# A decoder block on one core: at the end of a plain weight group, the next operands' preparation is queued behind the operation that empties the group's first bank, and one operand fewer is loaded ahead there

## The chip, the cores and the metric

The kernel runs on one core of a Trainium2 chip. The metric is the device time of one execution in microseconds (us), the median of three runs. Engines are named as in the profile: PE is TensorE (matmuls), DVE is VectorE, ACT is ScalarE, POOL is GpSimd, SP is the engine that issues the weight transfers.

## The reference, cut to what matters

One decoder block over 256 tokens of width 2048, all in float32: a norm, one combined input projection, two mixers (gated linear attention in 4 heads, a gated short convolution) whose outputs are gated and merged, an output projection, and a gated feed-forward part of width 5632, both with a residual.

```python
h = rmsnorm(x, mix_norm_w)
q, k, v, g_out, gk_low, gate_b, gate_c, xc, merge_a, merge_b = split(h @ w_in)
y_a = rmsnorm(gla_chunked(q, k, v, log_g)) * silu(g_out)          # per head
y_b = gate_b * causal_depthwise_conv(gate_c * xc, conv_w)
x = x + (sigmoid(merge_a) * y_a + sigmoid(merge_b) * y_b) @ w_out
gate, up = split(rmsnorm(x, ffn_norm_w) @ w_gate_up)
x = x + (silu(gate) * up) @ w_down
out = rmsnorm(x, final_norm_w)
```

## The kernel before, in words

**Arithmetic.** Every float32 operand is split into a high part hi (rounded to the format fp32r) and a remainder lo, and each product of two operands is three matmuls: lo with hi, hi with lo, hi with hi (`mm3`, lines 366 to 370; the profile's rows at L368, L369 and L370). The 256 tokens are two tiles of 128, t = 0 and t = 1; a matmul has one token tile's activations as weights and 512 output columns of the weight matrix as the moving operand. One such 512-wide matmul starts 0.23 us after the one before.

**Pieces.** The weight matrices come in pieces of 512 KB (128 x 1024 numbers). `load_piece` traces for one piece its transfer on SP (L253 or L316), the cast to hi on ACT (`high`, L259) and, one piece later, the subtraction that gives lo on DVE (`low`, L264). PE needs both before it can start on the piece.

**Groups.** Weight blocks go in two kinds of groups. A plain group (`eights`; `down` for the down projection) takes the pieces as they are: each piece is multiplied first with token tile 0 (6 matmuls into one PSUM bank), then with token tile 1 (6 matmuls into another). A sevens group (`sevens`) takes two blocks together and gets along with 7 products in place of 8; for that DVE also adds blocks of weights (L280 raw<-y,x; L286 x<-x,...; a cast and a subtraction follow for such a sum as for any piece) and in the end combines five banks (v, u at L446 to L460). The pieces of a plain group and of a sevens group take turns in the stream.

**Names of groups.** In the mixer part: q, k, v; g, ma, gb, mb with a column block 0 to 3 for the gates (g_out, merge_a, gate_b, merge_b, all plain groups), gc for the sevens of gate_c with xc. Then wo0 to wo3 (output projection), fg and fu (gate and up, blocks 0 to 10; blocks 3 to 7, 9 and 10 in sevens, the others plain), dn0_0 to dn3_4 (down projection; the first number is the part of the hidden width, the second the column block).

**Banks.** Five of the eight PSUM banks belong to the sevens. The three others ("lent") go round among the plain groups: a group takes two and gives them back at its end. Its successor so gets the third bank for t = 0, and for t = 1 the bank that held the predecessor's t = 0. The successor's first matmul for t = 1, which comes 6 matmuls after its first for t = 0, has to wait until that bank has been emptied. What empties a bank is the group's `done`: a silu on ACT for g (L1024), a sigmoid on ACT and a multiplication on DVE for ma and mb (L1014, L1015), an addition to the residual on DVE for wo and, in `down`, for dn (L1199), a silu on ACT for fg (L1155), a multiplication on DVE for fu (L1158).

**Order.** Within an engine the scheduler sets the order by the place at which an operation is traced, by its own estimate of when operands are there, and by explicit constraints. `take` (line 356) is called for each piece in the order of the stream: it traces the loading of further pieces until LOOK = 5 beyond the piece that is used, then the piece's matmuls are traced. So the preparation of later pieces stands in the trace ahead of the `done` of the group whose last piece is being used. There are 5 buffers for raw, 6 for hi, 5 for lo, 2 for x and 1 for y.

Of the kernel before, what the change touches and what calls it, by code (L numbers as in the profile page):

```python
# [12 lines left out]
ALU = mybir.AluOpType  # L13
# [55 lines left out]
PARTS = ((0, 3), (3, 6), (6, 9), (9, 11))  # L69
# [122 lines left out]
def stream_list():  # L192

    pieces = [(p[0], p[3]) for p in piece_list()]
    out = [e for e in pieces if e[0] in ("k0", "q0", "v0")] + heads_list() + gates_list()
    out += [e for e in pieces if e[0] == "wo0"]
    return out + hidden_list() + down_list()
# [3 lines left out]
def block_kernel(ctx, tc, x, xt, cols_in, gkw_in, gku_in, gnw, conv_w, finw, w_in, w_out, w_gu, w_dn, out):  # L201
    nc = tc.nc
# [12 lines left out]
    def bank(shape, name, tag=None):  # L215

        if tag is None:
            tag = f"b{turn['b'] % turn['of']}"
            turn["b"] += 1
        return psum.tile(shape, F32, tag=tag, name=name)  # L220
# [16 lines left out]
    LOOK = 5  # L237
    stream = stream_list()
# [6 lines left out]
    count = {"loaded": 0, "used": 0, "tick": 0}  # L245
    pending = []
    held = {}
# [8 lines left out]
    def high(raw, piece, a=0, b=None):  # L256
        hi, n = piece[0], piece[2]
        ks = slice(a, b or n)
        nc.scalar.copy(hi[:, ks, :], raw[:, ks, :])  # L259

    def low(raw, piece, a=0, b=None):
        hi, lo, n = piece
        ks = slice(a, b or n)
        nc.vector.tensor_tensor(out=lo[:, ks, :], in0=raw[:, ks, :], in1=hi[:, ks, :].bitcast(F32), op=ALU.subtract)  # L264

    def sum_of(pair, what, q):

        one, two = pair
        if what == "21":
            return fetch(one, 4 * q + 2)  # L270
        if what == "22":
            return fetch(two, 4 * q + 2)
        if what == "11":
            held["y"] = fetch(one, 4 * q, held["pool"], "y")
            return held["y"]
        y = held["y"]
        if what == "t1":
            held["x"] = fetch(two, 4 * q, held["pool"], "x")
            raw = wraw.tile([P, 2, 512], F32, tag="raw", name="raw")
            nc.vector.tensor_tensor(out=raw, in0=y, in1=held["x"], op=ALU.add)  # L280
            return raw
        x = held["x"]
        if halfway and halfway[-1][0] is x:
            finish_low()
        other = y if what == "t2" else fetch(two if what == "t3" else one, 4 * q + 2)
        nc.vector.tensor_tensor(out=x, in0=x, in1=other, op=ALU.add)  # L286
        return x

    def load_piece():


        i = count["loaded"]
        count["loaded"] += 1
        if i < len(stream):
            key, k0 = stream[i]
            if isinstance(k0, tuple):
                n, w = 2, 512
                raw = sum_of(key, *k0)
                step = n
            else:  # L300
                mat, j, n, w = index[(key, k0)]
                raw = wraw.tile([P, n, w], F32, tag="raw", name="raw")

                step = n // 2 if i < 2 else n
            piece = [whi.tile([P, n, w], F32R, tag="hi", name="hi"), None, n]
            if isinstance(k0, tuple):
                high(raw, piece)
                halfway.append((raw, piece, key, k0))
            else:
                if i < 2:  # L310
                    piece[1] = wlo.tile([P, n, w], F32R, tag="lo", name="lo")
                for a in range(0, n, step):
                    b = a + step
                    if (i, a) in hooks:
                        hooks.pop((i, a))()
                    nc.sync.dma_start(  # L316
                        raw[:, a:b, :], mats[mat][j, :, a * w:b * w].rearrange("p (k c) -> p k c", c=w))
                    high(raw, piece, a, b)
                    if i < 2:
                        low(raw, piece, a, b)  # L320
                if i < 2:
                    ready[(key, k0)] = piece
                else:
                    halfway.append((raw, piece, key, k0))
        if len(halfway) > 1 or (halfway and i >= len(stream)):
            finish_low()

    def finish_low():
        raw, piece, key, k0 = halfway.pop(0)
        piece[1] = wlo.tile([P, piece[2], PIECE // piece[2]], F32R, tag="lo", name="lo")  # L330
        low(raw, piece)
        ready[(key, k0)] = piece
# [19 lines left out]
    def one_at_a_time(delay, fn):  # L352

        spaced.append((count["tick"] + delay, fn))

    def take(key, k0):
        while count["loaded"] <= len(stream) and count["loaded"] <= count["used"] + LOOK:
            load_piece()
        return ready.pop((key, k0))

    def used(n=1):
        count["used"] += n
        for _ in range(n):
            tick()
# [7 lines left out]
    def tok_piece(ps, t, piece, k0, first, last, a):  # L372
        hi, lo, n = piece
        for k in range(n):
            ah, al = a(t, k0 + k)
            mm3(ps, ah, al, hi[:, k, :], lo[:, k, :], first and k == 0, last and k == n - 1)
# [19 lines left out]
    def eights(key, a, done, tags=None):  # L396

        mine = tags or [lent.pop(0) for _ in range(NT)]
        ps = [bank([P, 512], f"{key}_{t}", tag) for t, tag in enumerate(mine)]
        for k0 in range(0, KC, 2):  # L400
            piece, _ = yield
            for t in range(NT):
                tok_piece(ps[t], t, piece, k0, k0 == 0, k0 == KC - 2, a)

                if k0 == KC - 2:
                    done(t, ps[t])
        if tags is None:
            lent.extend(mine)

# [664 lines left out]
    order = heads_list()  # L1074
# [86 lines left out]
    order = hidden_list()  # L1161
# [25 lines left out]
    def down(key):  # L1187

        part, n = (int(s) for s in key[2:].split("_"))
        cs = slice(DOWN[part][n][0], sum(DOWN[part][n]))  # L1190
        mine = [lent.pop(0) for _ in range(NT)]
        ps = [bank([P, cs.stop - cs.start], f"{key}_{t}", tag) for t, tag in enumerate(mine)]
        number = sum(e[0] == key for e in order)
        for i in range(number):
            piece, k0 = yield
            for t in range(NT):
                tok_piece(ps[t], t, piece, k0, i == 0, i == number - 1, hidden_act(part))
                if i == number - 1:
                    nc.vector.tensor_tensor(out=h[:, t, cs], in0=ps[t], in1=h[:, t, cs], op=ALU.add)  # L1199
        lent.extend(mine)  # L1200

    def hidden(key):
# [41 lines left out]
    order = down_list()  # L1244
# [15 lines left out]
    for e in order:  # L1260
        key, k0 = e
# [85 lines left out]
```

## Time and profile before

| | before |
|---|---|
| median of 3 runs | 1505.42 us (1503.13 to 1505.94) |
| the profiled execution | 1505.51 us, its span 1503.7 us |
| PE busy | 1485.7 us, 99% of the span |
| DVE busy | 1310.4 us, 87% |
| ACT busy | 873.3 us, 58% |
| DMA | 241 GB/s on average |
| TensorE clock granted | full in all 40 slices |

Lines of the profile give an operation's line in the kernel, its engine, its tile "out<-in" without buffer numbers, the shapes, how many there are and how long they took; "idle before <-X" says how long the engine stood before it and what ended that. A timeline row begins with the start and the length in us from the start of the span; rows of one kind that follow directly on each other are one row, with x2 and their common length. A matmul's length in the timeline (0.39 us) is longer than the distance to the next, since matmuls overlap. The span of 1503.7 us is the profiled part; 1.8 us of the execution's 1505.51 lie around it.

### The profile page before, as it was taken

What the parts mean: (1) busy time and instruction counts of PE and PEld (TensorE: products, weight loads), DVE (VectorE), ACT (ScalarE), POOL (GpSimd) and SP (SyncE); (2) the same over time, 40 slices, a digit from 0 to 9 for tenths busy, and PEclk for the clock granted to TensorE, in tenths of its full rate; (3) what the DMA queues carried; (4) which work ended last, traced back from release to release, by engine and by line L of the source; (5) the groups of instructions that cost most, each with busy time, mean ns of one, the idle gap of its engine ahead of it and who ended that gap; (6) DMA issues with size and microseconds to landing.
All of it is one profiled execution on the core that took longest, in us unless ns stands there. A gap on an engine that the chain in (4) does not pass through costs nothing.

```text
span 1503.7 us, 19400 instructions
## 1 busy us (share of the span) xinstructions
PE 1485.7 (99%) x7040; PEld 1239.4 (82%) x7040; DVE 1310.4 (87%) x1314; ACT 873.3 (58%) x993; POOL 33.0 (2%) x59
## 2 busy tenths in 40 slices
PE   9999999999999999999999999999999999999998
PEld 8989988888788788888888888888888788888887
DVE  7898878978988989966789999999998999999975
ACT  7755565654565565554556756655564556565553
POOL 0010000001001001000000000000000000000000
PEclk9999999999999999999999999999999999999999
DMA  9666677787786778787666777876776878787782
GB/s 352 216 184 184 200 231 254 244 264 225 239 294 207 269 263 268 259 274 212 216 218 213 239 249 251 254 260 222 271 239 226 264 253 277 238 268 230 231 299 93
DMA packets 101280, 362.78 MB, mean 241 GB/s; under 512 B 11620, under 2 KB 11748, under 8 KB 101056
## 3 DMA queue, kind: packets, MB, share of 16 engines
q1 hardware_dynamic: 97808, 350.92, 71.4%
q0 software_dynamic: 2800, 8.89, 2.3%
q10 hardware_dynamic: 576, 1.72, 0.3%
q8 instruction: 55, 0.90, 0.2%
q14 instruction: 41, 0.34, 0.1%
HBM read 355.23 MB, written 2.10 MB: 238 GB/s over the span
## 4 chain that ended last, share of the span: by engine, by line
PE 88%; DVE 6%; issue 3%; DMA 2%; ACT 1%; SPq 0%; DVEq 0%; ACTq 0%
PE fg L368 8%; PE fg L370 8%; PE fg L369 8%; PE dn L368 5%; PE dn L370 5%; PE dn L369 5%; PE gc L368 3%; PE gc L370 3%; PE gc L369 3%; DVE lo L264 2%; DMA raw<-in_w_in_dram 2%; PE wo L368 2%; PE gb L368 2%; PE wo L370 2%; PE wo L369 2%
## 5 line engine op out<-in xcount | busy, mean ns | idle before, releaser
L264 DVE TENSOR_TENSOR lo<-raw,hi 128x1024 fp32r<-128x1024 f32 (+1 forms) x502 | 608.5, 1219 | 93.4 <-ACT hi L259 17.9
L259 ACT CAST hi<-raw 128x1024 fp32r<-128x1024 f32 (+1 forms) x502 | 519.8, 1047 | 229.5 <-PE mb L370 30.2
L259 ACT CAST hi<-x 128x1024 fp32r<-128x1024 f32 x156 | 164.2, 1053 | 314.3 <-DVE x L286 239.9
L264 DVE TENSOR_TENSOR lo<-x,hi 128x1024 fp32r<-128x1024 f32 x156 | 190.8, 1223 | 38.7 <-ACT hi L259 27.3
L368 PE MATMUL dn<-lo,acth 128*128 128x512 f32 (+1 forms) x368 | 140.9, 383 | 3.2 <-DVE h L1199 2.4
L286 DVE TENSOR_TENSOR x<-x,raw 128x1024 f32<-128x1024 f32 x104 | 126.8, 1220 | 16.0 <-DMA raw<-in_w_in_dram 10.3
L370 PE MATMUL dn<-hi,acth 128*128 128x512 f32 (+1 forms) x368 | 139.9, 380 | 0.0
L369 PE MATMUL dn<-hi,actl 128*128 128x512 f32 (+1 forms) x368 | 139.9, 380 | 0.0
L368 PE MATMUL fg<-lo,hh 128*128 128x512 f32 x288 | 112.5, 391 | 0.1
L370 PE MATMUL fg<-hi,hh 128*128 128x512 f32 x288 | 112.2, 390 | 0.0
L369 PE MATMUL fg<-hi,hl 128*128 128x512 f32 x288 | 112.2, 389 | 0.0
L368 PE MATMUL fg<-lo,sh 128*128 128x512 f32 x256 | 101.0, 395 | 0.0
L369 PE MATMUL fg<-hi,sl 128*128 128x512 f32 x256 | 99.9, 390 | 0.0
L370 PE MATMUL fg<-hi,sh 128*128 128x512 f32 x256 | 99.8, 390 | 0.0
L368 PEld LDWEIGHTS dn<-lo,acth 128*128 128x128 f32 x368 | 69.2, 188 | 17.7 <-DVE h L1199 3.9
L370 PEld LDWEIGHTS dn<-hi,acth 128*128 128x128 f32 x368 | 69.2, 188 | 13.3
L369 PEld LDWEIGHTS dn<-hi,actl 128*128 128x128 f32 x368 | 69.2, 188 | 12.9
L280 DVE TENSOR_TENSOR raw<-y,x 128x1024 f32<-128x1024 f32 x52 | 63.4, 1219 | 3.3 <-DMA y<-in_w_gu_dram 2.9
L264 DVE TENSOR_TENSOR lo<-y,hi 128x1024 fp32r<-128x1024 f32 x52 | 63.4, 1219 | 3.1 <-PE g L368 1.5
L368 PEld LDWEIGHTS fg<-lo,hh 128*128 128x128 f32 x288 | 54.1, 188 | 12.3 <-DVE lo L264 1.1
L286 DVE TENSOR_TENSOR x<-x,y 128x1024 f32<-128x1024 f32 x52 | 63.4, 1220 | 0.6
L370 PEld LDWEIGHTS fg<-hi,hh 128*128 128x128 f32 x288 | 54.1, 188 | 11.2
(269 smaller groups left out, 3053.9 us busy)
## 6 DMA issues: line engine op xcount, KB each, us to landing
raw<-in_w_in_dram SPq DMA_DIRECT2D x254, 512.0 KB, 4.7
raw<-in_w_gu_dram SPq DMA_DIRECT2D x176, 512.0 KB, 4.5
raw<-in_w_dn_dram SPq DMA_DIRECT2D x88, 512.0 KB, 4.6
y<-in_w_gu_dram SPq DMA_DIRECT2D x32, 512.0 KB, 4.3
x<-in_w_gu_dram SPq DMA_DIRECT2D x32, 512.0 KB, 4.8
raw<-in_w_out_dram SPq DMA_DIRECT2D x32, 512.0 KB, 4.0
y<-in_w_in_dram SPq DMA_DIRECT2D x20, 512.0 KB, 3.7
x<-in_w_in_dram SPq DMA_DIRECT2D x20, 512.0 KB, 6.0
```

The costliest lines, as they stand in the source:

```text
L259: nc.scalar.copy(hi[:, ks, :], raw[:, ks, :])
L264: nc.vector.tensor_tensor(out=lo[:, ks, :], in0=raw[:, ks, :], in1=hi[:, ks, :].bitcast(F32), op=ALU.subtract)
L280: nc.vector.tensor_tensor(out=raw, in0=y, in1=held["x"], op=ALU.add)
L286: nc.vector.tensor_tensor(out=x, in0=x, in1=other, op=ALU.add)
L368: nc.tensor.matmul(ps, lhsT=sh, rhs=ml, start=first, stop=False, skip_group_check=onto)
L369: nc.tensor.matmul(ps, lhsT=sl, rhs=mh, start=False, stop=False, skip_group_check=onto)
L370: nc.tensor.matmul(ps, lhsT=sh, rhs=mh, start=False, stop=last, skip_group_check=onto)
```

## The change

Three things, all in the order in which work is handed to the engines:

1. `ends` holds the places in the stream at which a plain group's last piece is used (v1; all g, ma, gb, mb; wo1 to wo3; the plain fg and fu; dn0, dn1, dn2; not wo0, not dn3). When `take` serves one of these, it loads ahead to LOOK − 1 pieces in place of LOOK. So one piece's preparation that was traced before the group's last matmuls and its `done` is traced at the next `take`, after them.
2. `emptying` calls `done` and, for token tile 0, notes the last DVE and the last ACT instruction that it traced.
3. The next `take` traces its preparations under `tc.issue_after` of these instructions: on the engine concerned, they are queued behind the noted one.

`down` has its addition in a function `added`, and passes it through `emptying`.

```diff
+    ends = {}
+    for i, (key, k0) in enumerate(stream):
+        if not isinstance(key, tuple) and (key[0] in "gm" or key == "v1" or key[:2] in ("wo", "fg", "fu", "dn")):
+            ends[key] = i
+    ends = {i for key, i in ends.items() if key != "wo0" and key[:3] != f"dn{len(PARTS) - 1}"}
+
     def take(key, k0):
-        while count["loaded"] <= len(stream) and count["loaded"] <= count["used"] + LOOK:
-            load_piece()
+
+        look = LOOK - (count["used"] in ends)
+        with ExitStack() as order:
+            for ins in held.pop("emptied", ()):
+                order.enter_context(tc.issue_after(ins))
+            while count["loaded"] <= len(stream) and count["loaded"] <= count["used"] + look:
+                load_piece()
         return ready.pop((key, k0))
+
+    def emptying(done, t, ps):
+
+        traced = nc.cur_bb.bb.instructions
+        last = traced[-1]
+        done(t, ps)
+        if t == 0:
+            start = next(k for k in reversed(range(len(traced))) if traced[k] is last) + 1
+            new = {i.engine: i for i in traced[start:]}
+            held["emptied"] = [new[e] for e in (mybir.EngineType.DVE, mybir.EngineType.Activation) if e in new]
...
-                    done(t, ps[t])
+                    emptying(done, t, ps[t])
...
+        def added(t, ps):
+            nc.vector.tensor_tensor(out=h[:, t, cs], in0=ps, in1=h[:, t, cs], op=ALU.add)
+
         for i in range(number):
...
                 if i == number - 1:
-                    nc.vector.tensor_tensor(out=h[:, t, cs], in0=ps[t], in1=h[:, t, cs], op=ALU.add)
+                    emptying(added, t, ps[t])
```

What that does to DVE's order at three group ends. The lines of the changed kernel are higher from `take` on (L460 is L482, L1015 is L1037, L1158 is L1180, L1199 is L1218), and a tile that is allocated later has another number (lo_3333 is lo_3355).

DVE at the end of mb0 (345 to 357 us of the profile), before. The sb rows are the multiplications with mb's sigmoid, for t = 0 and t = 1.

```order
L264 TENSOR_TENSOR lo_3307<-raw_3284,hi_3285 128x1024
L264 TENSOR_TENSOR lo_3333<-x_3270,hi_3305 128x1024
L460 TENSOR_TENSOR u_3030<-gc0_1_2527,v2_2531 128x512
L286 TENSOR_TENSOR x_3270<-x_3270,y_3252 128x1024
L1052 SCALAR_TENSOR_TENSOR u_3030<-gc0_0_2526,r1sq_121,u_3030 128x512
L264 TENSOR_TENSOR lo_3360<-raw_3329,hi_3330 128x1024
L1015 TENSOR_TENSOR sb_3079<-sb_3079,mb0_0_3100 128x512
L1015 TENSOR_TENSOR sb_3079<-sb_3079,mb0_1_3101 128x512
L264 TENSOR_TENSOR lo_3372<-x_3270,hi_3358 128x1024
```

The same place after:

```order
L264 TENSOR_TENSOR lo_3307<-raw_3284,hi_3285 128x1024
L482 TENSOR_TENSOR u_3030<-gc0_1_2521,v2_2525 128x512
L1074 SCALAR_TENSOR_TENSOR u_3030<-gc0_0_2520,r1sq_121,u_3030 128x512
L1037 TENSOR_TENSOR sb_3073<-sb_3073,mb0_0_3100 128x512
L1037 TENSOR_TENSOR sb_3073<-sb_3073,mb0_1_3101 128x512
L264 TENSOR_TENSOR lo_3355<-x_3270,hi_3305 128x1024
L264 TENSOR_TENSOR lo_3360<-raw_3351,hi_3352 128x1024
L286 TENSOR_TENSOR x_3270<-x_3270,y_3252 128x1024
L264 TENSOR_TENSOR lo_3372<-x_3270,hi_3358 128x1024
```

Both multiplications now stand ahead of two subtractions and of the x sum, and the x sum directly ahead of the subtraction that needs its cast.

DVE in fg7 (1275 to 1285 us), before. u1 and sg7 are the end of the sevens fg7 (t = 0 of its product), actl the low part of the activations that come from transposing sg7 on PE (trb).

```order
L264 TENSOR_TENSOR lo_10834<-raw_10818,hi_10820 128x1024
L286 TENSOR_TENSOR x_10816<-x_10816,raw_10842 128x1024
L264 TENSOR_TENSOR lo_10847<-raw_10830,hi_10831 128x1024
L264 TENSOR_TENSOR lo_10859<-x_10816,hi_10845 128x1024
L460 TENSOR_TENSOR u1_10867<-fg7_1_10193,v2_10197 128x512
L286 TENSOR_TENSOR x_10816<-x_10816,y_10804 128x1024
L1158 SCALAR_TENSOR_TENSOR sg7_10191<-u1_10867,r2_6375,sg7_10191 128x512
L264 TENSOR_TENSOR lo_10881<-raw_10855,hi_10856 128x1024
```

The same place after:

```order
L264 TENSOR_TENSOR lo_10834<-raw_10818,hi_10820 128x1024
L482 TENSOR_TENSOR u1_10867<-fg7_1_10193,v2_10197 128x512
L1180 SCALAR_TENSOR_TENSOR sg7_10191<-u1_10867,r2_6375,sg7_10191 128x512
L264 TENSOR_TENSOR lo_10847<-raw_10830,hi_10831 128x1024
L286 TENSOR_TENSOR x_10816<-x_10816,raw_10842 128x1024
L651 TENSOR_TENSOR actl_10784<-trb_10920,acth_10783 128x4x128
L264 TENSOR_TENSOR lo_10859<-x_10816,hi_10845 128x1024
L264 TENSOR_TENSOR lo_10881<-raw_10855,hi_10856 128x1024
```

u1 and sg7 stand ahead of two subtractions, and actl, which before came further down, ahead of the second of them. On PE the four transposes trb, before behind the last matmuls of the fg8 piece of lo_10847, now stand ahead of them.

DVE at the end of dn2_0 (1359 to 1368 us), before. The h rows add the two banks of dn2_0 to the residual.

```order
L264 TENSOR_TENSOR lo_11526<-raw_11509,hi_11510 128x1024
L286 TENSOR_TENSOR x_11495<-x_11495,raw_11521 128x1024
L460 TENSOR_TENSOR u1_11546<-fg9_1_10873,v2_10877 128x512
L1158 SCALAR_TENSOR_TENSOR sg7_10871<-u1_11546,r2_6375,sg7_10871 128x512
L264 TENSOR_TENSOR lo_11538<-x_11495,hi_11524 128x1024
L264 TENSOR_TENSOR lo_11560<-raw_11534,hi_11535 128x1024
L286 TENSOR_TENSOR x_11495<-x_11495,y_11483 128x1024
L1199 TENSOR_TENSOR h_6352<-dn2_0_0_11257,h_6352 128x512
L1199 TENSOR_TENSOR h_6352<-dn2_0_1_11258,h_6352 128x512
```

The same place after:

```order
L482 TENSOR_TENSOR u1_11546<-fg9_1_10873,v2_10877 128x512
L264 TENSOR_TENSOR lo_11526<-raw_11509,hi_11510 128x1024
L286 TENSOR_TENSOR x_11495<-x_11495,raw_11521 128x1024
L1180 SCALAR_TENSOR_TENSOR sg7_10871<-u1_11546,r2_6375,sg7_10871 128x512
L1218 TENSOR_TENSOR h_6352<-dn2_0_0_11257,h_6352 128x512
L264 TENSOR_TENSOR lo_11538<-x_11495,hi_11524 128x1024
L264 TENSOR_TENSOR lo_11560<-raw_11534,hi_11535 128x1024
L286 TENSOR_TENSOR x_11495<-x_11495,y_11483 128x1024
L1218 TENSOR_TENSOR h_6352<-dn2_0_1_11258,h_6352 128x512
```

The addition of t = 0 stands ahead of two subtractions and an x sum, u1 ahead of one subtraction; the addition of t = 1 stays behind the x sum.

## The prediction

> **What bounds the kernel now.** I read the page first, then what TensorE (PE) waited for, then the timeline around each wait. The first part of the page gives each engine's busy time:
>
> ```profile
> PE 1485.7 (99%) x7040; PEld 1239.4 (82%) x7040; DVE 1310.4 (87%) x1314; ACT 873.3 (58%) x993; POOL 33.0 (2%) x59
> ```
>
> The span is 1503.7 us, so a change of order alone, which takes no matmul away, can win only the time in which PE stands. The view of PE's waits (line waited for, its releaser: total, times, longest) says how much that is:
>
> ```profile
> PE dn L368 <- DVE h L1199: 2.4, 2, 1.9
> PE gc L368 <- DVE lo L264: 1.6, 3, 0.8
> PE ma L368 <- ACT ya L1024: 1.6, 1, 1.6
> PE gb L368 <- DVE ya L1015: 1.2, 1, 1.2
> PE dn L368 <- DVE lo L264: 0.8, 1, 0.8
> ```
>
> Three rows are waits for a PSUM bank to be emptied (h, ya, ya), the ones that the change is about: 2.4 + 1.6 + 1.2 = 5.2 us, 0.35% of the run. The two rows with lo are of another kind: the weight's low part, made by VectorE (DVE), wasn't ready. How the kinds lie to each other is seen in PE's timeline (start, length, idle before in brackets):
>
> ```profile
> 389.95 0.50 PE L368 MATMUL gb<-lo,xh 128*128 128x512 f32 x1 [1.21 <-DVE ya L1015]
> ...
> 400.77 0.50 PE L368 MATMUL gc<-lo,xh 128*128 128x512 f32 x1 [0.81 <-DVE lo L264]
> ...
> 497.50 0.50 PE L368 MATMUL ma<-lo,xh 128*128 128x512 f32 x1 [1.58 <-ACT ya L1024]
> ...
> 507.87 0.50 PE L368 MATMUL gc<-lo,xh 128*128 128x512 f32 x1 [0.56 <-DVE lo L264]
> ...
> 1177.36 0.50 PE L368 MATMUL dn<-lo,acth 128*128 128x512 f32 x1 [1.93 <-DVE h L1199]
> ...
> 1199.73 0.50 PE L368 MATMUL dn<-lo,acth 128*128 128x512 f32 x1 [0.76 <-DVE lo L264]
> ...
> 1422.51 0.50 PE L368 MATMUL dn<-lo,acth 128*128 128x512 f32 x1 [0.47 <-DVE h L1199]
> ```
>
> Each of the three long bank waits is followed, 10 to 22 us on, by a wait on lo. So in these stretches DVE, not the bank, says when PE goes on: had PE not stood for the bank, it would have stood that much longer for lo. Only the fourth wait, at 1422.51, has no such row behind it.
>
> **The change part by part.** Matmuls, casts, subtractions and transfers are the same; no operation is added. What moves is the order on DVE and ScalarE (ACT): at a plain group's end the operation that empties bank 0 (and with it, what the scheduler had ready) comes ahead of one to three preparations. SP's transfers keep nearly the order they have, since each waits for its buffer anyway, so I cost the one load fewer at nothing; where preparations are ahead of PE by several us, at most of the group ends, the move costs nothing either. DVE and ACT start what they have in the order of their queues (no row of the timeline is ahead of one queued before it), so what is moved ahead and has to wait for PE delays all preparation behind it. I go through the ends behind which lo is less than about 4 us ahead of PE.
>
> *End of mb0 (344 to 401 us).* The multiplication with mb's sigmoid (both token tiles) now stands ahead of two lo and an x sum.
>
> ```profile
> 348.40 1.24 ACT L1014 ACTIVATE mb<-mb,r 128x512 f32<-128x512 f32 x2
> 349.56 1.05 ACT L259 CAST hi<-x 128x1024 fp32r<-128x1024 f32 x1
> ...
> 350.43 1.28 DVE L1015 TENSOR_TENSOR sb<-sb,mb 128x512 f32<-128x512 f32 x2
> 351.63 1.22 DVE L264 TENSOR_TENSOR lo<-x,hi 128x1024 fp32r<-128x1024 f32 x1
> ...
> 360.35 1.23 DVE L999 TENSOR_TENSOR u<-u,taps 128x1024 f32<-128x1024 f32 x1 [1.68 <-DMA u<-u]
> ...
> 384.67 1.23 DVE L286 TENSOR_TENSOR x<-x,raw 128x1024 f32<-128x1024 f32 x1 [1.37 <-DMA raw<-in_w_in_dram]
> ...
> 399.50 1.22 DVE L264 TENSOR_TENSOR lo<-x,hi 128x1024 fp32r<-128x1024 f32 x1
> ```
>
> The sigmoids end at 348.40 + 1.24 = 349.64; the second multiplication (1.28 for both) ends some 0.65 later, at 350.3; two lo and the x sum (1.2 each) take 3.6, to 353.9; the cast of that x 1.05; so the lo that stood at 351.63 starts at about 354.9, 3.3 late. The idle 1.68 at 360.35 (a transfer not moved) swallows 1.7 of it; 1.6 go on. From 384.67 to 399.50 DVE has 14 rows with no idle between, and the lo at 399.50 ends 0.05 us ahead of the matmul at 400.77 that waits for it. So PE is there late by what is left: 0 if the transfer at 384.67 lands when it did, 1.4 if it comes as much later as its buffer does. I take +1.0, nearer to the second, as buffers are freed by the delayed engines. The 1.21 at 389.95 goes, and is waited for at 400.77.
>
> *End of g2 (497.50).* The same, with the delay covered by the convolution's transfers: 1.58 goes, lo at 507.87 gives it back. −0.2 (0 to −0.5).
>
> *End of dn0_0 (1010 to 1043).* A sevens' u (it waits for the last fg matmul) moves ahead of a lo:
>
> ```profile
> 1029.13 0.39 PE L370 MATMUL fg<-hi,sh 128*128 128x512 f32 x1
> ...
> 1028.63 1.23 DVE L264 TENSOR_TENSOR lo<-raw,hi 128x1024 fp32r<-128x1024 f32 x1 [0.29 <-ACT hi L259]
> ...
> 1030.91 0.68 DVE L460 TENSOR_TENSOR u<-fg,v 128x512 f32<-128x512 f32 x1
> ...
> 1041.67 1.23 DVE L264 TENSOR_TENSOR lo<-x,hi 128x1024 fp32r<-128x1024 f32 x1
> ...
> 1042.96 0.49 PE L368 MATMUL fg<-lo,hh 128*128 128x512 f32 x1
> ```
>
> u starts at 1029.13 + 0.39 = 1029.52, the lo behind it 0.6 later, at 1030.2 instead of 1028.63: 1.5 late; u's own 0.6 is saved further on, but the cast behind the x sum, which u used to cover, now stands open for 0.4: 1.3 late. The lo at 1041.67 ends at 1042.90, 0.06 ahead of its matmul: +1.2 (0.5 if a part is caught up).
>
> *End of dn1_1 (1177).* h moves ahead of one lo and an x sum, and the lo for which PE waited at 1199.73 ahead of an x sum and sg:
>
> ```profile
> 1209.05 1.23 DVE L264 TENSOR_TENSOR lo<-x,hi 128x1024 fp32r<-128x1024 f32 x1
> ...
> 1210.76 0.39 PE L368 MATMUL fg<-lo,hh 128*128 128x512 f32 x1
> ```
>
> So both waits go, 1.93 + 0.76 = 2.7 at 1199.73. But DVE has no less to do, and from there to 1210 hardly a gap: the lo of 1209.05 ends at 1210.28, 0.5 ahead of its matmul at 1210.76. PE can't keep more than that: −0.5 (0 if that lo comes later by the sums' moves, −1.9 if DVE wins time). The Trainium skill ("Perfetto Trace Analysis", Optimization Strategy) says to find the gaps of the engine that matters and make what it waits for start sooner. By it this gap alone would give the whole 1.9, and the sum would be 1.4 lower; the row at 1210.76 speaks against it here.
>
> *End of fg7's first half and of dn1_3 (1240 to 1294).* Now u and sg stand ahead of a lo, and actl (it waits for transposes of sg on PE and for a cast on ACT) ahead of the next:
>
> ```profile
> 1279.01 0.39 PE L370 MATMUL fg<-hi,sh 128*128 128x512 f32 x1
> 1284.68 0.60 PE L626 MATMUL trb<-ident,sg 128*128 128x128 f32 x4
> 1293.33 0.39 PE L368 MATMUL fg<-lo,hh 128*128 128x512 f32 x1
> ...
> 1278.60 1.22 DVE L264 TENSOR_TENSOR lo<-raw,hi 128x1024 fp32r<-128x1024 f32 x1
> 1279.86 1.23 DVE L264 TENSOR_TENSOR lo<-x,hi 128x1024 fp32r<-128x1024 f32 x1
> 1282.74 0.75 DVE L1158 SCALAR_TENSOR_TENSOR sg<-u,r,sg 128x512 f32<-128x512 f32 x1
> 1289.67 1.22 DVE L264 TENSOR_TENSOR lo<-x,hi 128x1024 fp32r<-128x1024 f32 x1
> ...
> 1278.77 1.06 ACT L259 CAST hi<-x 128x1024 fp32r<-128x1024 f32 x1 [1.37 <-DVE x L286]
> ```
>
> u can't start before 1279.40; with u 0.6 and sg 0.7 the lo of 1278.60 starts at 1280.7, 2.1 late. The x sum behind it ends at 1283.1, the cast (1.06, behind the one of the transposes, which PE now does ahead of fg8's piece) at 1284.2: the lo of 1279.86 is 4.3 late. From there to the lo of 1289.67 took 9.8; u, sg and actl are gone from it (−1.9), an open cast comes in (+1.1): it starts at 1293.2 and ends at 1294.4, where PE wants it at 1293.33: +1.1. If DVE comes to this place late already (v2 and v3 moved ahead 20 us earlier, by up to 3 us), it is +2.3. I take +1.5 (0.5 to 2.3).
>
> *End of dn2_0 (1360 to 1374).* h stands ahead of the lo of 1362.96:
>
> ```profile
> 1364.01 0.39 PE L370 MATMUL dn<-hi,acth 128*128 128x512 f32 x1
> 1374.26 0.40 PE L368 MATMUL fg<-lo,hh 128*128 128x512 f32 x1
> ...
> 1362.96 1.22 DVE L264 TENSOR_TENSOR lo<-x,hi 128x1024 fp32r<-128x1024 f32 x1
> 1366.37 1.28 DVE L1199 TENSOR_TENSOR h<-dn,h 128x512 f32<-128x512 f32 x2
> 1372.83 1.23 DVE L264 TENSOR_TENSOR lo<-x,hi 128x1024 fp32r<-128x1024 f32 x1
> ```
>
> The bank's last matmul ends at 1364.40, h takes 0.6: that lo starts at 1365.1, 2.1 late. Further on h's 0.6 is saved; 1.5 late, the lo of 1372.83 ends at 1375.6, where PE had 0.2 in hand: +1.3 (0.5 to 1.4).
>
> *End of dn2_2 (1422.51).* No lo is short behind it: the 0.47 goes, −0.5.
>
> *Absorbed.* PE that comes later waits less for lo where DVE is the late one for reasons of its own: of the 0.81 at 400.77 and 0.56 at 507.87, both behind the delay at mb0, I take −0.5 (0 to −1.0).
>
> Sum: 1.0 − 0.2 + 1.2 − 0.5 + 1.5 + 1.3 − 0.5 − 0.5 = +3.3. The profiled execution took 1505.51 (span 1503.7 and 1.8 around it), 0.1 from the median 1505.42: 1505.5 + 3.3 = 1508.8. With all lows (0, −0.5, 0.5, −1.9, 0.5, 0.5, −0.5, −1.0) it is −2.4, with all highs (1.4, 0, 1.3, 0, 2.3, 1.4, 0, 0) +6.4.
>
> **The rivals.** 0.2%, about what a measurement of this kernel can tell from no change, is 3.0 us: 1502.4 to 1508.4.
>
> *The bank waits are won for good* (the other side). It decides at the lo of 400.77, 507.87 and 1210.76: if these come as much sooner as PE does, because DVE fills its idle stretches (13% of the span) with them, all of 5.2 goes, and if the moved operations find PE done, nothing is lost: 1500.3. With 1 or 2 us of the losses it is 1501.3 to 1502.3. For it speaks that DVE has such idle time; against it that DVE has almost none in the 16 us before 400.77. The Trainium skill ("Perfetto Trace Analysis", Matmuls) has the emptying of one bank overlap the next group's matmuls where groups rotate through banks. Chance 0.19.
>
> *It cancels*: the bank waits come back as lo waits, and the operations moved ahead are mostly swallowed by idle DVE time as at 360.35: gains of 0.2 + 0.5 + 0.5 against 1 or 2 of loss, 1505.3 to 1506.3; with what is unclear of each, 1504 to 1507. Chance 0.21.
>
> *The load held back is late*: a transfer issued one piece later lands when a lo needs it (row 384.67 shows 1.37 of such a wait), at three ends on top of the forecast: about 1513. Against it: the order of SP hardly changes. Chance 0.06. That the change doesn't do what it says is excluded by the order of DVE.
>
> **How the numbers follow.** The forecast, that DVE's lost time is worth more than the banks, has the remaining 0.54: 1508.8, by itself from 1506 to 1511.9 (its lows belong to the rivals). Its middle lies 0.4 above the 1508.4, and its highs reach further than its lows: 0.34 of it above 1508.4, 0.20 within. So faster 0.19 (the first rival); same 0.20 + 0.21 = 0.41; slower 0.34 + 0.06 = 0.40. The range, 1501.5 to 1512.0, holds the forecast, the cancelling and the weaker half of the first rival; it leaves out that rival's full 1500.3 and the late loads.
>
> **What would show it.** Right: the rows with h and ya go from PE's waits and rows with lo grow, near 400, 1043, 1293 and 1374; DVE shows idle time ended by PE or ACT ahead of u, h, sg and actl there. Wrong: no lo row near 1293 and 1374 (then those terms fall), or PE earlier at 1210.76 by as much as it gained at 1177.36 (then the gains are kept).

## The result and the profile after

| | before | after |
|---|---|---|
| median | 1505.42 us (5 runs, 1503.13 to 1505.94) | 1512.43 us (5 runs, 1511.47 to 1514.46) |
| ratio (of the means, here and below) | | 1.0053, 95% interval 1.0038 to 1.0068 |
| the profiled execution | 1505.51, span 1503.7 | 1513.93, span 1512.2 |

The change costs 7.0 us by the medians (8.0 by the means), where I had forecast 3.3. The sign was right; the time lies 0.4 above the range. The engines' line of the page after:

```profile
PE 1489.4 (98%) x7040; PEld 1238.3 (82%) x7040; DVE 1305.2 (86%) x1314; ACT 869.0 (57%) x993; POOL 38.9 (3%) x59
```

As many instructions as before on PE, DVE and ACT, and DVE is busy 5.2 us less in a span that is 8.5 longer: it stands more. PE counts as busy 3.7 us longer for the same 7040 matmuls, so its rows of waits don't show the whole loss. PE's waits in the kernel after:

```profile
PE trb L648 <- DVE sg L1180: 3.5, 4, 1.3
PE fg L390 <- DVE lo L264: 3.5, 10, 0.8
PE gc L390 <- DVE lo L264: 2.0, 4, 0.9
PE ma L390 <- DVE lo L264: 1.7, 2, 1.1
...
PE gb L390 <- DVE lo L264: 0.8, 1, 0.8
```

All three rows of bank waits (h, ya, ya) are gone, and most of what came is waits for lo, as forecast; the row with trb (transposes), 3.5 us in four waits for sg, was in no term of mine. The rows of PE's timeline after that answer to those quoted before:

```profile
387.24 0.50 PE L390 MATMUL gb<-lo,xh 128*128 128x512 f32 x1 [0.79 <-DVE lo L264]
...
401.06 0.50 PE L390 MATMUL gc<-lo,xh 128*128 128x512 f32 x1 [0.86 <-DVE lo L264]
...
499.51 0.50 PE L390 MATMUL ma<-lo,xh 128*128 128x512 f32 x1 [1.12 <-DVE lo L264]
...
507.46 0.50 PE L390 MATMUL gc<-lo,xh 128*128 128x512 f32 x1 [0.39 <-DVE lo L264]
...
1042.46 0.51 PE L390 MATMUL fg<-lo,hh 128*128 128x512 f32 x1 [0.31 <-DVE lo L264]
...
1208.97 0.50 PE L390 MATMUL fg<-lo,hh 128*128 128x512 f32 x1 [0.25 <-DVE lo L264]
...
1296.21 0.50 PE L390 MATMUL fg<-lo,hh 128*128 128x512 f32 x1 [0.29 <-DVE lo L264]
...
1381.04 0.50 PE L390 MATMUL fg<-lo,hh 128*128 128x512 f32 x1 [0.29 <-DVE lo L264]
```

The same matmul stands in both traces, so the difference of its starts says how late PE is there: 400.77 became 401.06 (+0.3), 1042.96 became 1042.46 (−0.5), 1210.76 became 1208.97 (−1.8), 1293.33 became 1296.21 (+2.9), 1374.26 became 1381.04 (+6.8). I call this PE's shift, and took it for all matmuls, as a median over each 20 us (times of the trace of before):

| from, to | shift grows by | forecast |
|---|---|---|
| 340, 400 (end of mb0) | +1.0 | +1.0 |
| 1000, 1040 (end of dn0_0) | +1.4 | +1.2 |
| 1240, 1320 (fg7, end of dn1_3) | +4.7 | +1.5 |
| 1320, 1400 (end of dn2_0) | +4.0 | +1.3 |
| 1400, 1480 (dn2_2 and on) | +0.9 | −0.5 |
| all other stretches | −4.1 | −1.2 |

A step under about 1.5 can be read as the change's only where runs that leave the place alone show none: between 1160 and 1220 the shift falls by 0.7 to 1.5 in every run told of below, also where nothing is changed there. The two places from 1240 to 1400 make 8.7, more than the 7.9 that are left at the end.

What DVE lost there is read in the groups of its lo rows from 1236 to 1373 us (busy, mean ns, idle before them and its releasers), of before:

```profile
L264 DVE TENSOR_TENSOR lo<-raw,hi 128x1024 fp32r<-128x1024 f32 x46 | 55.8, 1219 | 2.5 <-PE dn L368 1.3 <-ACT hi L259 1.1
L264 DVE TENSOR_TENSOR lo<-x,hi 128x1024 fp32r<-128x1024 f32 x20 | 24.5, 1223 | 5.4 <-ACT hi L259 4.7 <-PE dn L368 0.3
```

and of the kernel after:

```profile
L264 DVE TENSOR_TENSOR lo<-raw,hi 128x1024 fp32r<-128x1024 f32 x45 | 54.4, 1218 | 2.1 <-ACT hi L259 1.9
L264 DVE TENSOR_TENSOR lo<-x,hi 128x1024 fp32r<-128x1024 f32 x18 | 22.0, 1224 | 11.5 <-ACT hi L259 11.3
```

The subtraction for an x sum needs that sum's cast, 1.05 us on ACT. If another operation of DVE stands between the sum and its subtraction, the cast is covered, by a short one in part; if none does, DVE stands for about 1.2 us. I call that an open cast. Added over all rows with idle time up to the same lo (1372.83 before, 6.9 later after), DVE stood 7.99 us before (10 rows) and 14.99 after (15 rows): 7.0 more, and it reaches that lo 6.9 later. So it isn't longer work that makes DVE late, but standing, and most of the increase is in waits for casts ahead of lo<-x (4.7 became 11.3). One such place, in DVE's timeline of before:

```profile
1247.24 1.22 DVE L286 TENSOR_TENSOR x<-x,raw 128x1024 f32<-128x1024 f32 x1
1248.38 1.22 DVE L264 TENSOR_TENSOR lo<-raw,hi 128x1024 fp32r<-128x1024 f32 x1
1249.66 1.23 DVE L264 TENSOR_TENSOR lo<-x,hi 128x1024 fp32r<-128x1024 f32 x1
```

and the same x sum after, with two more of the kind that the forecast spoke of, near 1290:

```profile
1248.88 1.23 DVE L264 TENSOR_TENSOR lo<-raw,hi 128x1024 fp32r<-128x1024 f32 x1 [1.53 <-ACT hi L259]
1250.02 1.22 DVE L286 TENSOR_TENSOR x<-x,raw 128x1024 f32<-128x1024 f32 x1
1252.41 1.22 DVE L264 TENSOR_TENSOR lo<-x,hi 128x1024 fp32r<-128x1024 f32 x1 [1.17 <-ACT hi L259]
...
1282.91 1.22 DVE L286 TENSOR_TENSOR x<-x,raw 128x1024 f32<-128x1024 f32 x1
1284.05 0.68 DVE L651 TENSOR_TENSOR actl<-trb,acth 128x512 fp32r<-128x512 f32 x1
1285.59 1.23 DVE L264 TENSOR_TENSOR lo<-x,hi 128x1024 fp32r<-128x1024 f32 x1 [0.85 <-ACT hi L259]
...
1287.86 1.22 DVE L286 TENSOR_TENSOR x<-x,y 128x1024 f32<-128x1024 f32 x1
1290.26 1.23 DVE L264 TENSOR_TENSOR lo<-x,hi 128x1024 fp32r<-128x1024 f32 x1 [1.18 <-ACT hi L259]
...
1343.22 1.23 DVE L264 TENSOR_TENSOR lo<-x,hi 128x1024 fp32r<-128x1024 f32 x1 [1.17 <-ACT hi L259]
```

The raw subtraction that stood behind the sum (1248.38) now stands ahead of it (1248.88), and the cast is open. The last row lies some 15 us behind the nearest group end, fu's near 1328; with dn1_3's end alone changed (a run below) the same cast is open 100 us behind that end. It is an order that the scheduler made anew; nothing in the change names it.

A second thing moved, on SP, whose order I had called nearly unchanged. SP's issues of before, and then of after:

```profile
1235.80 0.33 SPq L253 DMA_DIRECT2D y<-in_w_gu_dram  x1
1236.23 0.37 SPq L316 DMA_DIRECT2D raw<-in_w_gu_dram  x1
1239.35 0.33 SPq L253 DMA_DIRECT2D raw<-in_w_gu_dram  x1
1240.48 4.33 SPq L316 DMA_DIRECT2D raw<-in_w_gu_dram  x2
1244.87 0.42 SPq L253 DMA_DIRECT2D x<-in_w_gu_dram  x1
```

```profile
1235.57 0.33 SPq L253 DMA_DIRECT2D y<-in_w_gu_dram  x1
1242.68 0.33 SPq L253 DMA_DIRECT2D x<-in_w_gu_dram  x1
1243.06 0.42 SPq L316 DMA_DIRECT2D raw<-in_w_gu_dram  x1
1243.54 0.42 SPq L253 DMA_DIRECT2D raw<-in_w_gu_dram  x1
1244.00 1.02 SPq L316 DMA_DIRECT2D raw<-in_w_gu_dram  x2
```

An x transfer stands ahead of four raw transfers now. Its buffer is free only at 1242.68; SP issues nothing for 7.1 us, and the raws behind it start up to 6.8 us later. A cast of after that waits for one of them, on ACT, and delays the lo of 1248.88:

```profile
1247.79 1.05 ACT L259 CAST hi<-raw 128x1024 fp32r<-128x1024 f32 x1 [1.70 <-DMA raw<-in_w_gu_dram]
```

A second late raw delays a silu on ACT, and DVE stands at the sg that needs it:

```profile
1269.34 1.05 ACT L259 CAST hi<-raw 128x1024 fp32r<-128x1024 f32 x1 [2.81 <-DMA raw<-in_w_gu_dram]
...
1271.04 0.75 DVE L1180 SCALAR_TENSOR_TENSOR sg<-u,r,sg 128x512 f32<-128x512 f32 x1 [1.15 <-ACT sg L1177]
```

So the 7.0 us divide in two. Up to the lo of 1289.67 (1294.93 after) DVE stands 3.6 before and 8.3 after; of the 4.7 more, 2.0 are waits for casts of x sums (one more open cast, and 0.85 at 1285.59) and 2.7 are the two waits behind a late raw (1.53 and 1.15). From there to the lo of 1372.83 it stands 2.3 more: 4.5 of waits for casts of x sums and 1.0 of others came, and 3.2 of waits that the kernel before had there went.

### The profile page after: what moved, and what is told of

It is laid out like the page before. It is cut to its first block, busy times and chain, and to the rows that moved or that the text cites. A ratio compares the mean times of both kernels' runs of the same rounds, so it can differ in the third digit from the quotient of the medians.

```text
span 1512.2 us, 19373 instructions
## 1 busy us (share of the span) xinstructions
PE 1489.4 (98%) x7040; PEld 1238.3 (82%) x7040; DVE 1305.2 (86%) x1314; ACT 869.0 (57%) x993; POOL 38.9 (3%) x59
## 4 chain that ended last, share of the span: by engine, by line
PE 81%; DVE 9%; issue 4%; DMA 3%; ACT 2%; DVEq 0%; ACTq 0%; SPq 0%
PE fg L390 6%; PE fg L392 6%; PE fg L391 6%; DVE lo L264 5%; PE dn L390 4%; PE dn L392 4%; PE dn L391 4%; PE gc L390 3%; PE gc L391 3%; PE gc L392 3%; DVE x L286 3%; ACT hi L259 2%; PE wo L390 2%; PE wo L391 2%; PE wo L392 2%
```

## The experiments

Four theories came one after the other: the forecast's (what is moved at the group ends delays lo there), the order of the sevens' sums in fg7 on DVE, the x transfer that is ahead on SP, and the open casts. Under each expectation stands the measured median in us, with the ratio and its 95% interval. Each ratio is to runs of the kernel before on the same chip; shifts are as above, "fg7" from 1240 to 1320 and "dn2_0" from 1320 to 1400.

**Which part, which ends.** Either half of the change alone, then one part of the ends alone. With `ends` cut down, the constraint holds only for the ends that are left.

```diff
-        look = LOOK - (count["used"] in ends)
+        look = LOOK
```

> The queueing behind the emptying operation stays at every group end, but five pieces are loaded ahead everywhere, as before. If the loss comes from DVE standing at the operation that was moved ahead (and from what the scheduler reorders with it), most of it stays: 1508 to 1513 us. If it comes from the piece that is held back, it goes: 1503 to 1506 us.

1514.60, ratio 1.0057 (1.0045 to 1.0069). The other half, without the constraint:

```diff
-            held["emptied"] = [new[e] for e in (mybir.EngineType.DVE, mybir.EngineType.Activation) if e in new]
+            held["unused"] = [new[e] for e in (mybir.EngineType.DVE, mybir.EngineType.Activation) if e in new]
```

> One piece fewer is loaded ahead at the group ends, and nothing is queued behind the emptying operation by a constraint. If the loss comes from DVE standing at the moved operation by the constraint: 1503 to 1507 us. If it comes from the piece that is held back (its preparation is traced after the group's end, which alone puts the emptying operation ahead of it): 1509 to 1513 us.

1512.45, 1.0039 (1.0027 to 1.0051). Either half alone makes the loss. Then the ends:

```diff
+    chosen = [key for key in ends if key[0] in "gm" or key == "v1"]
```

> Both parts of the change, at the ends of v1 and of the gates' groups alone (up to 760 us of the profile). If the loss lies in the feed-forward part, as PE's shift between the two profiles says (-1.1 us at 740, +7.9 at the end): 1503.5 to 1506 us, with PE as in the changed kernel up to 740. If it lies in the mixer part (the forecast's +1.0 at 400): 1506 to 1508 us.

1503.38, 0.9984 (0.9975 to 0.9992).

```diff
+    chosen = [key for key in ends if key[:2] in ("wo", "fg", "fu", "dn") and key != "wo0" and key[:3] != f"dn{len(PARTS) - 1}"]
```

> Both parts of the change, at the ends of wo, fg, fu and dn alone (from 760 us on). If the loss lies in the feed-forward part: 1511 to 1515 us. If it lies in the mixer part, or if both parts are needed for it: 1504 to 1508 us.

1516.48, 1.0071 (1.0059 to 1.0083). The mixer's ends gain a little, the loss is behind them. One end alone, all but two, and fg and fu alone:

```diff
+    ends = {i for key, i in ends.items() if key == "dn1_3"}
```

> Both parts of the change at the end of dn1_3 alone. In DVE's order this end alone moves everything between 1250 and 1370 us that the whole change moves there: v, u, sg and actl of fg7 and the addition of dn2_0. If the loss of 1220 to 1400 comes from these operations, moved along by the scheduler far behind the end itself: 1511 to 1514.5 us. If each end costs by its own moved addition: at most 1507 us.

1510.61, 1.0039 (1.0025 to 1.0053); fg7 +4.5, dn2_0 +2.4.

```diff
+    ends = {i for key, i in ends.items() if ... and key not in ("dn1_2", "dn1_3")}
```

> The whole change but for the ends of dn1_2 and dn1_3. The order of fg7 is then nearly that of before, that of dn2_0 (its addition ahead of two lo, u ahead of a lo) is still that of the change. If fg7's part costs 4.7 us and dn2_0's 3.9 us, as PE's shift says: 1507 to 1509 us. If dn2_0's delay comes only with a DVE that is late already: 1503 to 1506 us.

1507.41, 1.0016 (1.0007 to 1.0025); fg7 +0.4, dn2_0 +3.5.

```diff
+    ends = {i for key, i in ends.items() if key[:2] in ("fg", "fu")}
```

> The change at the ends of the plain fg and fu alone. Of what costs in the changed kernel it moves only the place of dn2_0: its addition and u ahead of lo, without the transposes that PE does earlier there. By the forecast's step +1.3: 1506 to 1507.5 us; by PE's shift of 3.9 between the profiles: 1508.5 to 1510 us.

1507.66, 1.0020 (1.0009 to 1.0030); fg7 0, dn2_0 +2.2. So the one end of dn1_3 is enough for fg7's loss, and it loses also 100 us behind itself; the ends of fg and fu have a loss at dn2_0 of their own.

**What the bank waits were worth.** The four dn ends at which only the addition moves; v1's end; and a choice of ends at which little else moves, with and without the gates' (g, ma, gb, mb):

```diff
+    ends = {i for key, i in ends.items() if key in ("dn1_0", "dn1_1", "dn2_1", "dn2_2")}
```

> The change at dn1_0, dn1_1, dn2_1 and dn2_2 alone. If the wait at 1177 us is mostly given back and the one at 1422 won, as the forecast has it (-0.5 and -0.5): 1504 to 1505 us. If all bank waits of dn (2.4 us) are won: 1502.5 to 1503.5 us.

1505.97, 0.9995 (0.9986 to 1.0004). PE's waits in it:

```profile
PE trb L648 <- DVE sg L1180: 1.3, 2, 0.8
...
PE dn L390 <- DVE lo L264: 0.8, 1, 0.8
```

The 2.4 of dn <- h are gone, and the time is that of before. That doesn't show them given back, as the forecast had it, because most of them weren't there to win: in the traces of seven other kernels that leave dn1_1's end alone the wait of 1.93 at 1177.36 is 0.4 to 0.7 us, as here with one swap (last run below):

```profile
1177.69 0.50 PE L369 MATMUL dn<-lo,acth 128*128 128x512 f32 x1 [0.45 <-DVE h L1200]
```

So the long wait is that of the one execution profiled, and about 1.0 of the 2.4 is left, 0.07% of the time, which this interval can't tell from nothing. The shift's fall between 1160 and 1220 fits this too.

```diff
+    ends = {i for key, i in ends.items() if key == "v1"}
```

> The change at the end of v1 alone, where the profile before shows no wait for a bank. If what the mixer's ends gained (1503.38 us) is v1's: 1503 to 1504.5 us. If it is the gates': 1505 to 1506 us, as before.

1504.23, 0.9983 (0.9974 to 0.9992). The profile before shows no wait for a bank at v1's end.

```diff
+    ends = {i for key, i in ends.items() if (key[0] in "gm" or key == "v1") or (key[:2] == "wo" and key != "wo0") or key in ("dn1_0", "dn1_1", "dn2_1", "dn2_2")}
```

> The change at v1, all gates, wo1 to wo3 and dn1_0, dn1_1, dn2_1, dn2_2, where in the order nothing but the addition itself moves. If only the operations moved along cost time and the bank waits are won where lo is not short behind them: 1500 to 1503 us. If DVE takes every won bank wait back: 1503.5 to 1506 us.

1501.85 (11 runs, 1500.57 to 1503.10), 0.9977 (0.9968 to 0.9985): the fastest version, 3.5 us under the before of its own chip.

```diff
+    ends = {i for key, i in ends.items() if key == "v1" or (key[:2] == "wo" and key != "wo0") or key in ("dn1_0", "dn1_1", "dn2_1", "dn2_2")}
```

> The chosen ends (1501.85 us) without the gates: v1, wo1 to wo3, dn1_0, dn1_1, dn2_1, dn2_2. If the gates' bank waits are given back at lo, as the forecast has it: 1500.5 to 1503 us, as with them. If the gates' bank waits (1.6 and 1.2 us) are won: 1503.5 to 1505.5 us.

1503.81, 0.9984 (0.9975 to 0.9993): its interval overlaps the last one's, so the runs don't tell whether the 2.8 us that PE stood for ya are won or given back. v1's end alone has the same ratio as these ends together, so what the chosen ends win isn't shown to come from bank waits; why v1's end wins stays open.

**The order of the sums in fg7 and fg9.** The whole change, with v and u queued behind the last lo traced, as before:

```diff
+                    with behind_low(name):
+                        nc.vector.tensor_tensor(out=v2, in0=pc, in1=v2, op=ALU.subtract)
```

> The whole change, but in the sevens fg7 and fg9 the combining operations (v, u) are queued behind the last lo that is traced before them, which gives fg7's operations the places behind lo that they have in the kernel before. The additions of dn stay where the change puts them. If it is v, u, sg and the transposes moved ahead of lo that cost in fg7: 4 to 6 us less than the changed kernel, 1506 to 1508.5 us. If it is the moved additions of dn1_2 and dn1_3 themselves, or the load held back: 1511 to 1513.5 us.

1513.66, 1.0048 (1.0035 to 1.0061); fg7 +4.5. That theory fell.

**The x transfer on SP.** The whole change with the two x transfers back behind the raws that they had passed:

```diff
+        behind = {46: 462, 50: 494}.get(len(xs)) if tag == "x" else None
+        with ExitStack() as order:
+            if behind:
+                order.enter_context(tc.issue_after(raws[behind - 1]))
+            nc.sync.dma_start(raw, mats[mat][j].rearrange("p (k c) -> p k c", c=w))
```

> The whole change, but the two x transfers that it moved ahead of raw transfers on SP (near 1235 and 1330 us) are queued behind them. DVE's order stays that of the changed kernel at the ends and nearly so in fg7 and at dn2_0. If SP, standing at an x transfer with the raw ones behind it, makes the loss: 1503 to 1507 us. If the order on DVE makes it: 1510 to 1513.5 us.

1509.61, 1.0028 (1.0017 to 1.0040); fg7 +3.2, dn2_0 +4.3. In place of 1.0053, so it is a part of the loss, up to 2.8 us. In its trace the wait for the first late raw (1.53 on DVE) is gone, the second raw is still late (1.93 on ACT in place of 2.81). The reverse, the kernel before with that transfer issued four raws earlier (for that one sum it loads another weight block):

```diff
+            if tag == "raw" and len(raws) in range(458, 462):
+                order.enter_context(tc.issue_after(held["early"][1]))
```

> The kernel before, with the transfer of one x (that of fg9's first sums) traced and issued four raw transfers earlier, and these four queued behind it. No load is held back and nothing is queued behind an emptying operation. If SP's queue makes the loss: 1509 to 1512 us, 4 to 6 more than before. If the change's own moves make it: 1505 to 1506.5 us.

1511.97, 1.0038 (1.0024 to 1.0052); fg7 +4.5, dn2_0 +2.8. It looked like the whole cause. But with that transfer the scheduler also made its order on DVE anew, with as many open casts as in the change, so the run doesn't tell the two apart. The ends of fg and fu alone (1507.66 above) with their x transfer back:

```diff
+        behind = {50: 494}.get(len(xs)) if tag == "x" else None
```

> The change at the ends of fg and fu alone (1507.66 us), with the x transfer near 1330 us put back behind the raw ones. dn2_0's addition and u stay ahead of lo. If SP makes dn2_0's loss: 1504 to 1506 us. If it is the addition ahead of lo on DVE, as forecast (+1.3): 1506.5 to 1508 us.

1508.21, 1.0018 (1.0009 to 1.0027): nothing won, so dn2_0's loss isn't SP's. Both put back, the transfers and fg7's sums, in the whole change; then also without the ends of dn0_0 and dn2_0 and with fg9's u and dn2_0's addition back:

> The whole change with both put back: the two x transfers behind the raw ones on SP, and v and u of fg7 behind lo on DVE. dn0_0 and dn2_0 stay as the change has them. If SP's queue and fg7's operations ahead of lo are the loss of 4.7 us near 1240 to 1300 us: 1506.5 to 1508.5 us. If there is a third cause there: 1509 to 1512 us.

1510.37, 1.0036 (1.0025 to 1.0047); fg7 +3.6.

> As the run before it, and dn0_0's end left as in the kernel before, dn2_0's addition behind the lo that it stood behind before, and u of fg9 too. If the three places make up the loss: 1501.5 to 1504.5 us, as fast as the chosen ends (1501.85) or a little slower. If something else of the change costs: 1506 us or more.

1508.72, 1.0020 (1.0012 to 1.0029); dn0_0's +1.4 is gone, fg7 +3.7 and dn2_0 +3.4 stay. Nothing that I had named was left to explain them. The lo<-x group of the kernel with transfers and fg7's sums back, same window, showed what was:

```profile
L270 DVE TENSOR_TENSOR lo<-x,hi 128x1024 fp32r<-128x1024 f32 x18 | 22.0, 1224 | 12.4 <-ACT hi L265 12.1
```

No less idle than in the change itself.

**Open casts.** In DVE's order I counted, of the 20 x sums that stand from 1234 to 1371 us in the trace of before, those that are directly followed by the subtraction that waits for their cast:

| open of 20 | kernels, us |
|---|---|
| 4 | before 1505.4; chosen ends 1501.9, mixer 1503.4, no gates 1503.8, v1 1504.2, four dn 1506.0 |
| 6 | fg and fu 1507.7, with x back 1508.2 |
| 8 | without dn1_2 and dn1_3 1507.4, x back 1509.6, dn1_3 1510.6, x ahead 1512.0, the change 1512.4, look 1512.5, order 1514.6, FFN 1516.5 |
| 9 | all back 1508.7, x and fg7 back 1510.4, sums behind lo 1513.7 |

No kernel with 4 is over 1506.0, none with more is under 1507.4. The count doesn't give the time, though: with 8 it goes from 1507.4 to 1516.5. Nor does every open cast cost: over the whole kernel the traces show 15 before, 26 in the change and 21 in the chosen ends, the fastest, whose six more all lie ahead of 520 us. So the table is no proof, and the last run makes open casts by the smallest edit I found, in the kernel before: the subtraction of one piece is traced ahead of one x sum (the 130th), so that the two neighbours at 1247.24 and 1248.38 change places. The scheduler opens three more behind it.

```diff
+        held["sums"] = held.get("sums", 0) + 1
-        if halfway and halfway[-1][0] is x:
+        if halfway and (halfway[-1][0] is x or held["sums"] in (130,)):
             finish_low()
```

> The kernel before, with one thing changed: the x sum at 1247.24 us of its trace is traced behind the subtraction of the piece before it, so that these two neighbours change places on DVE and the subtraction that needs the sum's cast stands directly behind the sum. No constraint, no load held back, and no x transfer moves on SP (one y transfer goes behind one raw). In the order the scheduler then makes, 8 of 20 x sums from here to dn2_0's end are directly followed by the subtraction that needs their cast, as in the changed kernel, instead of 4. Theory of the open casts: each such place costs DVE about 1.17 us of idle time (the rows of the three in the trace of before: 1.17 to 1.19), four more are 4.7, of which 1 to 2 are lost in DVE's waits for PE near 1340; DVE's idle time from 1236 to the end of dn2_0 grows from 8.0 to 11 to 13 us, and the time is 1508.5 to 1511. Theory of the late transfers: what costs is that an x transfer stands ahead of four raw transfers on SP; it doesn't here, so no cast waits for a raw near 1248, and the time is that of before within 0.2%.

1510.53, 1.0032 (1.0021 to 1.0043). DVE's timeline at the swap, and its lo<-x group:

```profile
1246.47 2.35 DVE L264 TENSOR_TENSOR lo<-raw,hi 128x1024 fp32r<-128x1024 f32 x2
1248.74 1.22 DVE L287 TENSOR_TENSOR x<-x,raw 128x1024 f32<-128x1024 f32 x1
1251.15 1.22 DVE L264 TENSOR_TENSOR lo<-x,hi 128x1024 fp32r<-128x1024 f32 x1 [1.19 <-ACT hi L259]
```

```profile
L264 DVE TENSOR_TENSOR lo<-x,hi 128x1024 fp32r<-128x1024 f32 x19 | 23.2, 1223 | 10.0 <-ACT hi L259 9.8
```

Two neighbours of DVE in another order (and what the scheduler makes of it: three more open casts, one y transfer behind a raw), no constraint, no x transfer ahead, and the kernel is 5 us slower. DVE's idle time up to the same lo is 11.96 instead of 7.99, +4.0; PE's shift from 1240 to 1400 is +3.6. The theory of the late transfers forecast no change here: they aren't needed for a loss. But the 3.6 divide into +0.9 at fg7 and +2.7 at dn2_0, where the change has +4.7 and +4.0. So open casts are shown to make most of dn2_0's loss, where also fg and fu alone, with two more open, lost 2.2. Of fg7's, this run shows 0.9 and putting the x transfer back 1.5; the rest is argued from DVE's rows, not shown.

## Why the prediction was right or wrong

**Bank waits come back as waits for lo: right in the sum for the gates, not shown for dn.** The three rows are gone. For the gates 2.8 us of waits for ya went, and the waits of gc, ma and gb for lo grew from 1.9 to 4.5. They didn't grow where I had said: those at 400.77 and 507.87, 0.81 and 0.56, are 0.86 and 0.39 now, and what came is 1.12 at 499.51 and smaller ones. For dn about 1.0 of the 2.4 was there in other executions, and the time of the four ends doesn't decide about it. The rule of the Trainium skill ("Perfetto Trace Analysis", Optimization Strategy) to make start sooner what PE waits for, by which closing the gap at 1177.36 would have given 1.9, isn't tested by these runs for the same reason. The rival that all of the bank waits are won for good falls for the change as a whole; at the ends where little else moves 3.5 us were won, but v1's end alone, which I had costed at nothing, won as much within the noise.

**End of dn0_0: right, mechanism and size.** +1.4 for +1.2: u stands for PE and a part-open cast follows, as I had it, and that shift is 0 in the runs without dn0_0's end. It is 0 also with either half of the change alone, which leaves DVE's order there as it was.

**End of mb0: mechanism right, size not to be told.** On DVE the lo of 351.63 comes 3.0 later against what stood ahead of it (forecast 3.3), and behind the idle stretch at 360.35 there are 1.3 left (1.6). PE's shift grows by 1.0 as forecast, but it grows by 0.7 and 1.0 also in the runs with the feed-forward ends and with the four dn ends, which leave mb0's end alone.

**fg7 and dn1_3, dn2_0: the steps that failed.** I had +1.5 and +1.3 and measured +4.7 and +4.0. The step was to cost only what moves at the group's end itself (for fg7 "an open cast comes in (+1.1)", for dn2_0 only h) and to let the rest of the stretch run as before. In the trace DVE's own standing is the loss: from 1236 to the lo of 1372.83 it grows by 7.0: 6.5 more in waits for casts of x sums, where 4 whole open casts became 8 and others opened in part, 2.7 behind late raws and 1.0 in others, less 3.2 that went. I had priced the kind rightly, 1.1 for one (measured 1.17 to 1.20), and counted one where there are several. By DVE's rows the lo of 1289.67, which I had 3.5 late, comes 5.3 late, with the two late raws in it, which no term had. My sum then had PE 2.8 late in all at 1374.26, that is, it let DVE win back 2.0 of the 3.5 before dn2_0; in the trace nothing is won back, since new open casts stand where DVE had idle time to spare. The lo of 1372.83 comes 6.9 late and its matmul 6.8. The open casts could be counted blind: the order of DVE shows which x sum is directly followed by its own subtraction. One swap of two neighbours, with what the scheduler makes of it, costs 5 us.

**SP's transfers "keep nearly the order they have, since each waits for its buffer anyway": wrong.** Because they wait for buffers, a transfer that is moved ahead holds back those behind it, 7.1 us here. Putting it back took fg7 from +4.7 to +3.2 and the time from 1512.43 to 1509.61, so it is the smaller part. The rival of the late load, which gave 1513, named a neighbour of this mechanism; that it comes so near the time is luck, since a loss of 5 us comes with no x transfer moved.

**trb.** Transposes moved ahead on PE wait for sg (1.3 longest); no term had that. At 1271.04 sg waits for ACT, whose silu stands behind a cast that waits for a raw. Two of the four waits, 1.5 us, lie between 1240 and 1400; the fastest version has 1.5 us of such waits too. What these 3.5 us alone cost was not tried.

**dn1_1, g2, dn2_2, absorbed (together −1.7): not to be told.** The shifts there are within what runs of unchanged order show. Together with all that had no term (v1's end among it) PE gained 4.1 outside the places named, where I had 1.2; without that the sum would have been further off, so that it missed its range by only 0.4 is partly luck.

Open stays why the scheduler, after a change at one place, puts later sums directly ahead of their subtractions; its estimates aren't in a trace. Open also stay the part of fg7's loss that no run shows alone, and what v1's end wins. Closing the four open casts of before was not tried.

## What to carry to other kernels

On an engine that is nearly full, look at each pair of operations between which another engine has a step to do, and count how many have nothing in between: each makes the engine stand for the whole step (here 1.2 us), and where what it feeds has no time in hand they add up. Elsewhere they can cost nothing: the fastest version has 21 of them, the kernel before 15. When a scheduler sets the order, a constraint at one place gives a new order far behind it, so compare the whole order, not the place; then keep the constraint only where little else moves (1501.85 here, for 1512.43 with all). A queue that issues in order stands at a transfer whose buffer isn't free: a transfer that is moved ahead is not free of cost because it would wait anyway.

## What the runs showed of the hardware that I had not expected

SP stood 7.1 us at one x transfer, and the raw transfers behind it, three of which the kernel before issues 3.5 to 6.8 us earlier, were not issued until it was. A busy ACT isn't needed for its latency to count: at 57% busy, its 1.05 us casts add 6.5 us to the time that DVE stands.
